# Reading the samples' states out four pairs of heads at a time instead of two

## The chip, the cores and the metric

The kernel runs on one core of a Trainium2 chip. The metric is the device time of one execution in microseconds (us): the median of the runs of a kernel on the chip. Times of single instructions come from one profiled execution.

## The reference, cut to what matters

The program is one step of a hybrid decoder layer, for a prompt of 1024 tokens and for 8 samples of 8 tokens each. It projects the normalised input, mixes one part over windows, passes the other through a state-space recurrence (SSD) with 32 heads in 4 groups, and joins both. The change concerns only the recurrence of the samples. For them a chunk is the 8 tokens of a sample, and the state that comes in is not zero:

```python
# per sample b, group g, head e (8 heads of a group share B and C); p: 64, n: 128
acs   = cumsum(dt * A)                                     # over the sample's 8 tokens
y     = einsum('bijge,bjgep->bigep', att, x)               # within the sample
y     = y + einsum('bign,bige,bgepn->bigep', C, exp(acs), h)     # read-out of the state h
last  = acs[:, -1]
w_in  = exp(last - acs) * dt
h     = h * exp(last) + einsum('bjgn,bjge,bjgep->bgepn', B, w_in, x)   # update of the state
```

The state h has 8 samples x 32 heads x 64 x 128 numbers (8.4 MB). Every state is read from memory once, read out with C, updated, and written back.

## The kernel before, in words

**The frame.** The weight products (gemms) are computed by a Strassen-like scheme. One `product` is twice 12 matmuls of 272 columns (L614) into a PSUM buffer `ps` or `mm`. The weights come in as tiles `rawA`, loaded on SP's queue; sums and differences of weight blocks are formed at L546, on DVE or on POOL (GpSimd); then each block is split into a high part `whi` (L165, ScalarE, that is ACT) and a low part `wlo` (L168, POOL), which go to the matmuls. Results are added up by DVE (L623), copied as `s` by ACT (L655), or passed through a sigmoid as `u` (L730) and stored as `gp` (L732).

**The samples' part** is the class `Samples`, one object for each of the 4 groups of 8 heads. A group's states come in 8 tiles `h`, j = 0 to 7: j divided by 4 says which four of the samples (the half), j modulo 4 which pair of heads. Each tile has 128 partitions (two heads x 64) and four blocks of 128 (four samples). For a tile there are these steps:

- `load_h0(j)`: load of the tile on SP's queue; there are four buffers.
- `turn(j)`: four transposes (L1309) into one PSUM buffer `ps` of four.
- `turned(j)`: ScalarE copies that to SBUF (L1314), into `hT` for an even j and `yt` for an odd one, one buffer each.
- `state(j)`: the read-out. For each of the four samples one matmul (L1323) takes the sample's C as weights (`cz`, 8 tokens padded to 32 columns) and the turned state, and writes 32 rows of the PSUM buffer `pc`. `pc` has one buffer, which takes the four pairs of a half side by side.
- `update(j)`: one matmul (L1332) of 96 rows and 512 columns gives what is added to the state, in a buffer `ps`; four DVE instructions (L1335) multiply the old state by its decay and add it, in place in `h`; the new state is stored from ACT's queue (L1337).

Once in a half, `out()` copies `pc` to SBUF (L1342, in the buffer `hT`), `end(hf)` turns it back and adds it to the result `t`, and `spread(hf)` and `split(hf)` (L1279 to L1293) prepare C, B and x for the four samples; the copy `cz` is among it (L1271). Once in a group, `decay()` masks the matrix `dec` on POOL (L1201, L1202) and takes eight exponentials of it on ScalarE (L1207), for which another function table is loaded than the one that the copies and the sigmoid use. `rows` (L1255 to L1257) and `within` give the part of the samples' own tokens.

**The order around it.** `all_samples()` is a generator that cuts these steps into 7 pieces for each group, with a `yield` between two. The pieces are put between the products of the last ten gemm units, at some pace (`samples_beside`, from L1658). PE (the matmul engine) and SP, whose queue does the loads, run in the order in which this is written; ACT, DVE and POOL run in an order that a scheduler makes when the program is built, from priorities and its own idea of when things are ready. The whole samples' part lies between about 600 and 800 us of the span. After it comes the recurrence of the prompt, and at the very end 16 loads on POOL's software queue that add the input to the result in memory (`plus_x`, L2048).

Of the kernel before, what the change touches and what calls it, by code (L numbers as in the profile page):

```python
# [20 lines left out]
P = 128  # L21
# [25 lines left out]
def tile_pool_ssd_step(  # L47
# [6 lines left out]
    nc = tc.nc  # L54
    uid = [0]

    def nm(s):
        uid[0] += 1
        return f"{s}_{uid[0]}"
# [177 lines left out]
    def x_copy(turned, eng):  # L237
        g3, k, px, c = turned
        o = BLK[g3][0]
        if eng is V:  # L240
            V.tensor_copy(tf[k][:, o:o + c], px[:, :c])
        else:
            act(tf[k][:, o:o + c], px[:, :c], AF.Copy)
# [981 lines left out]
    def spt(shape, tag, bufs, dt=F32):  # L1225
        return sp.tile(list(shape), dt, tag=tag, name=nm(tag), bufs=bufs)

    class Samples:
# [81 lines left out]
            self.pt[j] = pt  # L1310

        def turned(self, j):
            self.hts[j] = spt([P, 512], ("hT", "yt")[j % 2], 1)
            act(self.hts[j], self.pt.pop(j), AF.Copy)  # L1314

        def state(self, j):
# [40 lines left out]
    def all_samples():  # L1357
        gs_ = [Samples(g) for g in range(NG)]
        gs_[0].begin()
        gs_[0].decay()  # L1360
        for j in range(2):
            gs_[0].load_h0(j)
        yield
        gs_[0].rows()
        gs_[0].spread(0)
        yield
        gs_[0].split(0)
        yield
        for g, m in enumerate(gs_):
            n = gs_[g + 1] if g + 1 < NG else None  # L1370
            if g:
                gs_[g - 1].end(1)
            m.turn(0)
            m.turn(1)
            m.turned(0)
            m.turned(1)
            if g:
                m.split(0)
            m.within()
            m.load_h0(2)  # L1380
            m.load_h0(3)
            yield
            m.turn(2)
            m.turn(3)
            m.state(0)
            m.state(1)
            m.turned(2)
            m.turned(3)
            m.update(0)
            m.update(1)  # L1390
            m.load_h0(4)
            m.load_h0(5)
            yield
            m.state(2)
            m.state(3)
            m.out()
            m.update(2)
            m.update(3)
            m.spread(1)
            yield  # L1400
            m.end(0)
            m.turn(4)
            m.turn(5)
            m.turned(4)
            m.turned(5)
            m.split(1)
            m.load_h0(6)
            m.load_h0(7)
            if n:
                n.begin()  # L1410
            yield
            m.turn(6)
            m.turn(7)
            m.state(4)
            m.state(5)
            m.turned(6)
            m.turned(7)
            m.update(4)
            m.update(5)
            if n:  # L1420
                n.load_h0(0)
                n.load_h0(1)
                n.decay()
            yield
            if n:
                n.rows()
                n.spread(0)
            m.state(6)
            m.state(7)
            m.out()  # L1430
            m.update(6)
            m.update(7)
            yield
        gs_[-1].end(1)
        yield
# [220 lines left out]
    run_units(units, 1, lambda: next(pre, None))  # L1656
    banks_[0] = (PB, PA)
    side = all_samples()  # L1658
    due, made_ = [0.0], [0]
    FIRST = 14  # L1660
# [567 lines left out]
```

## Time and profile before

| | |
|---|---|
| runs of the kernel before | 1266.97, 1267.12, 1267.76 us; median 1267.12 |
| span of the profiled execution | 1265.2 us |
| its instructions | 26432 |
| busy: PE (matmul) | 1239.8 us, 98% |
| busy: PEld (weight load) | 1158.1 us, 92% |
| busy: DVE | 974.4 us, 77% |
| busy: ACT (ScalarE) | 682.6 us, 54% |
| busy: POOL (GpSimd) | 716.2 us, 57% |
| memory traffic | 171.26 MB read, 85.10 MB written, 203 GB/s over the span |

The span runs from the first to the last recorded instruction of the profiled execution. A run's time holds the launch too: the median of the runs is 1.9 us above the span. A line of the timeline gives the start in us from the span's start, the busy time in us, the engine, the source line, the operation with its output and inputs, its shape, and how many equal instructions in a row it stands for (x8); the busy time is that of the whole row. Square brackets at its end give an idle time ahead of it and the instruction that ended it. [...] A line of the waits gives who waited for what, the total idle time, the number of waits and the longest.

### The profile page before, as it was taken

The numbers are of one execution on the slowest core, as the hardware profiler recorded it, in microseconds if no ns is written. First come the engines' busy times: TensorE is split into PE (matmuls) and PEld (weight loads), VectorE is DVE, ScalarE is ACT, GpSimd is POOL, SyncE is SP. The second block draws the span as 40 slices with busy tenths as digits, with TensorE's granted clock in tenths as the row PEclk, the third lists the DMA queues.
The fourth block names the chain that finished last, engine by engine and source line by source line (L and its number), as shares of the span: only waits on it lengthen the run. The fifth ranks groups of instructions, "written<-read, shape, count | busy, mean of one in ns | idle before, by whom it ended". The sixth has DMA issues, their size and how long they took to land.

```text
span 1265.2 us, 26432 instructions
## 1 busy us (share of the span) xinstructions
PE 1239.8 (98%) x9679; PEld 1158.1 (92%) x9679; DVE 974.4 (77%) x1713; ACT 682.6 (54%) x1566; POOL 716.2 (57%) x607
## 2 busy tenths in 40 slices
PE   7999999999999999999999999999999999999997
PEld 6779999999999999999999989998888988999886
DVE  4686689986998598876676775488677988759986
ACT  4665347465556546455656554646676656401425
POOL 1006767886968777764444444354686877503662
PEclk9999999999999999999999999999999999999999
DMA  9836554564546545444666565998878887866884
GB/s 328 265 112 205 152 158 155 180 205 157 162 154 199 160 155 176 131 150 122 175 177 194 166 178 154 324 308 274 253 241 288 279 250 247 275 226 219 250 192 158
DMA packets 262499, 257.99 MB, mean 204 GB/s; under 512 B 29761, under 2 KB 200337, under 8 KB 262362
## 3 DMA queue, kind: packets, MB, share of 16 engines
q1 hardware_dynamic: 181632, 163.93, 42.7%
q10 hardware_dynamic: 78434, 88.18, 20.2%
q0 software_dynamic: 2304, 4.20, 1.8%
q8 instruction: 77, 1.26, 0.4%
q14 instruction: 52, 0.43, 0.1%
HBM read 171.26 MB, written 85.10 MB: 203 GB/s over the span
## 4 chain that ended last, share of the span: by engine, by line
PE 65%; DMA 2%; DVE 2%; ACT 1%; issue 1%; POOL 0%; SPq 0%; ACTq 0%; DVEq 0%
PE mm L358 17%; PE mm L614 14%; PE ps L614 14%; PE ps L1219 3%; PE pc L614 2%; PE pc L1541 2%; PE ps L1222 2%; PE ps L2023 2%; PE ps L2025 2%; PE ps L2024 2%; PE ps L1309 1%; PE ps L1516 1%; PE ps L1332 1%; PE pc L1323 1%; PE mm L2033 1%
## 5 line engine op out<-in xcount | busy, mean ns | idle before, releaser
L168 POOL TENSOR_TENSOR wlo<-rawA,whi 128x512 fp32r<-128x512 f32 x120 | 174.2, 1456 | 175.2 <-ACT whi L165 89.8
L168 POOL TENSOR_TENSOR wlo<-raw,whi 128x512 fp32r<-128x512 f32 x92 | 153.2, 1674 | 106.9 <-ACT whi L165 75.3
L358 PE MATMUL mm<-Y,whi 128*128 128x352 f32 (+1 forms) x960 | 196.2, 334 | 0.3 <-DVE Y L1579 0.3
L358 PEld LDWEIGHTS mm<-Y,whi 128*128 128x128 f32 x960 | 159.1, 188 | 6.6 <-issue 5.1
L1062 DVE SCALAR_TENSOR_TENSOR GA<-GA,cvT,GA 128x1112 f32<-128x1112 f32 x72 | 133.4, 1857 | 0.1
L614 PE MATMUL mm<-Y,whi 128*128 128x272 f32 x832 | 125.3, 292 | 1.5 <-DVE Y L484 1.1
L614 PE MATMUL ps<-Y,whi 128*128 128x272 f32 x832 | 122.4, 289 | 0.0
L165 ACT ACTIVATE whi<-rawA 128x512 fp32r<-128x512 f32 x125 | 78.1, 627 | 76.0 <-PE ps L614 42.1
L165 ACT ACTIVATE whi<-raw 128x512 fp32r<-128x512 f32 x96 | 59.4, 628 | 106.4 <-DVE raw L546 48.4
L614 PEld LDWEIGHTS mm<-Y,whi 128*128 128x128 f32 x832 | 112.1, 188 | 4.8 <-DVE Y L484 1.5
L614 PEld LDWEIGHTS ps<-Y,whi 128*128 128x128 f32 x832 | 110.9, 188 | 0.4
L1207 ACT ACTIVATE dec<-dec,acT 128x128 f32<-128x128 f32 (+1 forms) x288 | 86.9, 383 | 27.0 <-POOL dec L1198 26.4
L358 PE MATMUL mm<-Y,wlo 128*128 128x352 f32 (+1 forms) x480 | 98.7, 327 | 0.0
L358 PEld LDWEIGHTS mm<-Y,wlo 128*128 128x128 f32 x480 | 81.7, 188 | 0.0
L434 POOL TENSOR_TENSOR pw<-pw,ph 128x512 fp32r<-128x512 f32 x40 | 68.4, 1711 | 12.6 <-ACT ph L432 11.5
L614 PE MATMUL mm<-G,whi 128*128 128x272 f32 x496 | 73.4, 289 | 0.0
L614 PE MATMUL ps<-G,whi 128*128 128x272 f32 x496 | 72.6, 288 | 0.0
L614 PE MATMUL mm<-Y,wlo 128*128 128x272 f32 x416 | 69.3, 288 | 0.0
L614 PE MATMUL ps<-Y,wlo 128*128 128x272 f32 x416 | 69.2, 288 | 0.0
L614 PEld LDWEIGHTS mm<-G,whi 128*128 128x128 f32 x496 | 66.6, 189 | 0.7
L614 PEld LDWEIGHTS ps<-G,whi 128*128 128x128 f32 x496 | 66.3, 188 | 0.0
L1478 POOL TENSOR_TENSOR Y<-xb,Y 128x512 fp32r<-128x512 f32 x32 | 41.7, 1304 | 37.0 <-ACT Y L1476 37.0
(531 smaller groups left out, 3192.5 us busy)
## 6 DMA issues: line engine op xcount, KB each, us to landing
rawA<-in_w_in SPq DMA_DIRECT2D x62, 512.0 KB
dec<-acs_d SPq DMA_DIRECT2D x32, 512.0 KB
xbc<-GA ACTq DMA_DIRECT2D x24, 512.0 KB
Y<-wo SPq DMA_DIRECT2D x10, 1024.0 KB
pw<-in_w_ssm_out ACTq DMA_DIRECT2D x32, 256.0 KB
ws<-ph ACTq DMA_DIRECT2D x32, 256.0 KB
ws<-pw ACTq DMA_DIRECT2D x32, 256.0 KB
h<-in_state_ssm SPq DMA_DIRECT2D x32, 256.0 KB
```

The source lines that it names most:

```text
L165: ins = act(hi[:, :, :ncols], raw[:, :, :ncols], AF.Copy)
L168: (eng or nc.gpsimd).tensor_tensor(lo[:, :, :ncols], raw[:, :, :ncols], hi[:, :, :ncols].bitcast(F32), ALU.subtract)
L358: mm(ps[:, :n], w[k // 4][h][:, k % 4, :], r[k][:, o:o + n], start=(j == 0), stop=(j == len(terms) - 1))
L434: nc.gpsimd.tensor_tensor(raw.bitcast(F32R), raw, hi.bitcast(F32), ALU.subtract)
L614: mm(p, w[j // 8][:, k], A(k, s)[j // 4 == 1], start=(j == 0), stop=(j == 11))
L1062: V.scalar_tensor_tensor(d[:, :n], rp[:, k:k + n], cvT[:, 24 * k + mc:24 * k + mc + 1], d[:, :n], ALU.mult, ALU.add)
L1207: act(dec[:, h], dec[:, h], AF.Exp, bias=acT[:S, c, 8 * g + h:8 * g + h + 1], scale=-1.0)
L1219: mm(o[hh], xd[:S, 2 * q + hh, :], dec[:S, 2 * q + hh], start=True, stop=state is None)
L1222: mm(o[hh], state[:, h * 64:h * 64 + 64], cE[:, h], start=False, stop=True)
L1478: nc.gpsimd.tensor_tensor(yl[g][:, :, o:o + S], v, yhc.bitcast(F32), ALU.subtract)
L1541: mm(pu, bt, xw.rearrange("p h d -> p (h d)"), start=True, stop=True)
L2023: mm(ps, hi, y[:, k, c0:c0 + cw], start=(first and k == 0), stop=False)
```

## The change

There are four buffers of turned states instead of two: `turned(j)` takes `hT`, `yt`, `hU`, `hV` in turn. The read-out `state(j)` of the first two pairs of a half no longer stands between the transposes of the second two and their copies; it stands at the start of the next piece, together with that of the second two, so that 16 read-out matmuls follow one another. The two new buffers take 2 KB of each partition each; the scratch memory for transfers with software-made descriptors (those of POOL's software queue) goes from its 16384 bytes to 8192.

```diff
@@ turned(self, j)
-            self.hts[j] = spt([P, 512], ("hT", "yt")[j % 2], 1)
+            self.hts[j] = spt([P, 512], ("hT", "yt", "hU", "hV")[j % 4], 1)
             act(self.hts[j], self.pt.pop(j), AF.Copy)
@@ all_samples(), first half
             yield
             m.turn(2)
             m.turn(3)
-            m.state(0)
-            m.state(1)
             m.turned(2)
             m.turned(3)
             m.update(0)
...
             yield
-            m.state(2)
-            m.state(3)
+            for j in range(4):
+                m.state(j)
             m.out()
             m.update(2)
             m.update(3)
@@ all_samples(), second half
             yield
             m.turn(6)
             m.turn(7)
-            m.state(4)
-            m.state(5)
             m.turned(6)
             m.turned(7)
             m.update(4)
...
                 n.spread(0)
-            m.state(6)
-            m.state(7)
+            for j in range(4, 8):
+                m.state(j)
             m.out()
@@ kernel(**inputs)
-    nc = _bacc.Bacc("TRN2", target_bir_lowering=False, num_devices=1)
+    nc = _bacc.Bacc("TRN2", target_bir_lowering=False, num_devices=1, dynamic_dma_scratch_size=8192)
```

## The prediction

> **What bounds the kernel now.** I read the page first, then the busy time by stretch around the changed code, then who waited for whom on TensorE (PE) there, and last the timeline of single places.
>
> ```profile
> span 1265.2 us, 26432 instructions
> PE 1239.8 (98%) x9679; PEld 1158.1 (92%) x9679; DVE 974.4 (77%) x1713; ACT 682.6 (54%) x1566; POOL 716.2 (57%) x607
> 720.00:760.00 40.00, 38.27 (x352) 35.85 (x352) 29.59 (x70) 22.19 (x48) 18.21 (x15) 1.00 0.59 173
> PE ps L1332 <- ACT s L655: 2.0, 2, 1.7
> ```
>
> PE is busy for 98% of the span, so a microsecond of PE time is a microsecond of the end. The third row is one 40 us stretch of the part in which the samples' read-out runs (columns: length; PE, PEld, DVE, ACT, POOL busy; PE's granted clock): PE lacks 1.73 us there, and the fourth row, the waits of PE from 600 to 800 us, tells what for: PE waits in this whole part for one thing only, at L1332 (the update of the states) for ScalarE's copy `s` of L655, twice. So what counts is PE's own time, and these two places, which I call A (near 646 us, first group of heads) and C (near 735 us, third group). The three runs' median is 1267.12 us, 1.9 us over the span; I add my sum to the span and carry the 1.9 us along.
>
> **The change on PE.** There are 4 groups with two halves, so 8 places where the read-out of two pairs (L1323, 32 columns wide) disappears and 8 where it comes twice as long. A place of the first kind, PE's timeline at A, with the later one of the same half:
>
> ```profile
> 635.98 1.03 PE L1309 MATMUL ps<-ident,h 128*128 128x128 f32 x8
> 636.94 0.43 PE L1323 MATMUL pc<-hT,cz 128*32 128x128 f32 x8
> 637.18 0.40 PE L1323 MATMUL pc<-yt,cz 128*32 128x128 f32 x8
> 637.52 0.73 PE L1332 MATMUL ps<-dec 96*128 96x512 f32 x2
> 638.08 1.16 PE L614 MATMUL mm<-Y,whi 128*128 128x272 f32 x8
> ...
> 645.48 0.49 PE L1332 MATMUL ps<-dec 96*128 96x512 f32 x1
> 646.23 0.50 PE L1332 MATMUL ps<-dec 96*128 96x512 f32 x1 [0.25 <-ACT s L655]
> ```
>
> The eight transposes of L1309 start 0.108 us apart (1.03 less the 0.27 of one, by 7), the last at 636.74. From there to the next gemm matmul at 638.08 are 1.34 us. Without the read-out the update would follow the transposes at their pitch, about 0.11, and two matmuls of 512 columns stream at the gemm's rate: eight of 272 columns start (1.16 - 0.29) / 7 = 0.124 apart (0.29 is that of one), so 512 columns take 0.23, two 0.47. That is 0.57, and 0.77 us go. The difference holds two gaps at the change of array form, from 636.74 to 636.94 and from the last read-out, near 637.3, to 637.52. What comes back at the later place: sixteen narrow matmuls, which go four side by side; the first eight start 0.24 before the second eight (636.94 to 637.18), and at the transposes' pitch four more rounds take 4 x 0.108 = 0.43; bounds 0.43 and 0.48. Net 0.77 - 0.43 = 0.34 us gained in each half; 0.28 to 0.42 over the bounds, the upper one if a matmul follows a transpose at once. I take 0.34, by the pitches of the rows themselves.
>
> The freed 0.77 us only counts if the update isn't late for something else. Its second PSUM buffer was last read by ScalarE or VectorE after the gemm before it. The tightest of the eight places is the second group's first half:
>
> ```profile
> 658.82 0.43 DVE L623 TENSOR_TENSOR u<-u,ps 128x272 f32<-128x272 f32 x1
> 659.80 0.73 PE L1332 MATMUL ps<-dec 96*128 96x512 f32 x2
> ```
>
> The addition is over at 659.25. The second update matmul starts at 660.03 or later (the two take 0.73, one at most 0.50 by the rows above): 0.78 us of room, of which 0.77 are used up. If it doesn't fit, hundredths of a microsecond are lost. The buffers of the transposes are freed by ScalarE's two copies `turned`; these waited for the read-out (hT's and yt's old content) and now have buffers hU, hV of their own, so they come earlier.
>
> **The change on ScalarE.** PE and SP stand in the written order, ACT, DVE and POOL in the scheduler's. In the built program the new order on ACT differs at A and C in one thing that matters. Before: copies of the turned states, table load, seven exponentials `dec`, store of the updated state (`out<-h`), one exponential, second store. After: copies, **first store**, table load, eight exponentials, second store, and then as before the halving `whi`, the second table load, `u` twice, `s` of `mm`, `whi`, `s` of `ps`. The store is issued from ACT's queue and waits there for DVE's update L1335; behind it now stand the table load and all exponentials, and at the end the copy `s` that PE waits for. In the second group both stores stand ahead of the table load already, and PE doesn't wait there, where no copy `s` holds its buffer. ACT and DVE at A before:
>
> ```profile
> 638.59 1.28 ACT L1207 ACT_TABLE_LOAD   x1
> 639.88 0.35 ACT L1207 ACTIVATE dec<-dec,acT 64x64 f32<-64x64 f32 x1
> 639.99 0.40 ACTq L1337 DMA_DIRECT2D out<-h  x1
> ...
> 641.02 0.40 ACTq L1337 DMA_DIRECT2D out<-h  x1
> ...
> 641.82 0.62 ACT L165 ACTIVATE whi<-rawA 128x512 fp32r<-128x512 f32 x1
> 642.45 1.28 ACT L730 ACT_TABLE_LOAD   x1
> 643.75 0.75 ACT L730 ACTIVATE u<-u 128x272 f32<-128x272 f32 x2
> 644.52 0.34 ACTq L732 DMA_DIRECT2D gp<-u  x1
> 644.97 0.40 ACT L655 ACTIVATE s<-mm 128x272 f32<-128x272 f32 x1 [0.48 <-PE ps L1257]
> 645.26 0.62 ACT L165 ACTIVATE whi<-rawA 128x512 fp32r<-128x512 f32 x1
> 645.78 0.39 ACT L655 ACTIVATE s<-ps 128x272 f32<-128x272 f32 x1
> 636.53 2.39 DVE L546 TENSOR_TENSOR rawA<-rawA,rawA 128x512 f32<-128x512 f32 x1
> 638.85 2.14 DVE L1335 SCALAR_TENSOR_TENSOR h<-h,E,ps 128x128 f32<-128x128 f32 x8
> ```
>
> The store is issued at 639.99, when the first four of the eight L1335 are done, and its issue takes 0.40: the table load starts near 640.46 instead of 638.59. From there: load 1.28, eight exponentials 1.94 (639.88 to 641.82), `whi` 0.63 to the load, load 1.30, `u` twice 0.75 to 646.37. The store of `u` now stands behind `s` of `mm`, not ahead of it, so only `whi` waits for its issue: it starts 0.45 after `u` as `s` did (644.50 to 644.97), then 0.52 to `s` of `ps` and 0.39 for it. Sum 7.3 us: `s` ends at 647.76, and PE goes on 0.06 later (before: 645.78 + 0.39 to 646.23), at 647.8. That is **1.6 us later than now**, whatever PE saved on its way there. The DVE chain isn't moved: L1335 already waits for the addition L546, not for PE. At C:
>
> ```profile
> 729.36 0.40 ACTq L1337 DMA_DIRECT2D out<-h  x1
> 729.80 0.35 ACT L1207 ACTIVATE dec<-dec,acT 64x64 f32<-64x64 f32 x1 [0.53 <-DVE h L1335]
> 734.88 0.39 ACT L655 ACTIVATE s<-ps 128x272 f32<-128x272 f32 x1
> 721.65 0.86 DVE L546 TENSOR_TENSOR raw<-raw,rawA 128x512 f32<-128x512 f32 x1
> 724.14 4.15 DVE L546 TENSOR_TENSOR rawA<-rawA,rawA 128x512 f32<-128x512 f32 x1
> 728.21 2.14 DVE L1335 SCALAR_TENSOR_TENSOR h<-h,E,ps 128x128 f32<-128x128 f32 x8
> 733.09 0.49 PE L1332 MATMUL ps<-dec 96*128 96x512 f32 x1
> 735.32 0.50 PE L1332 MATMUL ps<-dec 96*128 96x512 f32 x1 [1.73 <-ACT s L655]
> 724.16 1.27 POOL L168 TENSOR_TENSOR wlo<-raw,whi 128x512 fp32r<-128x512 f32 x1
> 725.39 1.10 POOL L1202 TENSOR_SCALAR_AFFINE_SELECT dec<-dec 64x512 f32<-64x512 f32 x1
> 726.46 1.28 POOL L168 TENSOR_TENSOR wlo<-raw,whi 128x512 fp32r<-128x512 f32 x1
> 727.71 1.74 POOL L546 TENSOR_TENSOR raw<-raw,rawA 128x512 f32<-128x512 f32 x1
> ```
>
> One exponential already waits for the store here (the 0.53). The store at 729.36 puts the table load at 729.82, 7.3 us later `s` ends at 737.12, PE goes on at 737.2 instead of 735.32: **1.9 us later**.
>
> **The sum.** Six halves gain 0.34 each, -2.0 us; A +1.6, C +1.9: +1.5 us. 1265.2 + 1.5 + 1.9 = **1268.6 us**. The six other halves' savings pass on in full, as PE waits for nothing else there. The terms' bounds (0.28 to 0.42 for a half, 0.2 for each stall) give this case 1267.8 to 1269.3. Costed at nothing: the second store at A, which leaves near 642.05 instead of 641.02, behind the eighth exponential; SP's next load into that buffer waits for its landing, but PE needs it only after another product of 24 matmuls, and those are late by the same stall. The delayed `whi` of A and C feed products that come two and more later. On DVE the copy `cz` now stands ahead of L1335 at these places, behind the stall; only stores wait for that.
>
> The 8 KB scratch serves POOL's own transfers, the 16 adding loads `plus_x` at the very end (packets, MB, share of 16 engines):
>
> ```profile
> q0 software_dynamic: 2304, 4.20, 1.8%
> ```
>
> No row shows a wait for its space; if half of it were too little, transfers issued in a burst would wait for earlier ones to land. I take nothing.
>
> **Rivals.** (1) *The additions L546 come out short, and it gets faster.* The addition takes 0.86 us when left alone (721.65), 2.39 at A and 4.15 at C, where it starts as POOL begins an operation and ends only in POOL's fourth. If both were at 0.86, L1335 would start 1.5 us sooner at A and 3.3 sooner at C, and the chain behind it: A +0.1, C -1.4, in sum -3.3 and 1263.8 us. Against it: DVE and POOL keep their order up to there, and what starts them moves with PE alike.
>
> (1b) *The addition waits for one POOL operation only.*
>
> ```profile
> 635.96 1.27 POOL L168 TENSOR_TENSOR wlo<-raw,whi 128x512 fp32r<-128x512 f32 x1
> ```
>
> With the operation that runs when it comes (over at 637.23 at A, 725.43 at C) and its own 0.86 it would end at 638.09 and 726.29, 0.8 and 2.0 us sooner than in these rows: A +0.8, C -0.1, in sum -1.3 and 1265.8 us. Only the 4.15 at C, which outlasts three operations, speaks against it. [...]
>
> (2) *Slower: the addition at A takes as long as at C.* Then L1335 and the store come 1.76 us later there, and A costs 3.4 instead of 1.6: 1270.4 us. It decides from about 3.4 us of that addition on.
>
> (3) *Slower: PE cools down.* At C PE would stand idle from about 733.2 to 737.2, 4.0 us; now it is 1.73, with a clock of 1.00 in the stretch around it. If PE ran at half its rate for as long as the pause was, 2.0 us were lost: 1270.6 us. It decides from a length of pause between 1.73 and 4.0 us. [...]
>
> (4) *The scratch is too small.* POOL's loads at the end come late; slower by a few us.
>
> (5) *ACT isn't held by the store's wait*: eight halves gain 0.34, A and C stay as they are: 8 x 0.34 is -2.7, 1264.4 us, and less if ACT comes sooner too. The 0.53 us row at C speaks against it.
>
> **How the numbers follow.** 0.2% (2.5 us) is about what a measurement of this kernel can tell from no change: 1264.6 to 1269.7 counts as the same. Forecast 0.42, rival 1b and other mixed outcomes 0.10: same 0.52. Rival 2 0.15, rival 3 0.13, rival 4 0.03: slower 0.31. Rival 1 0.11, rival 5 0.06: faster 0.17. The range reaches from rival 1's 1263.8 less 0.4 for its terms' bounds to rival 3's 1270.6 with 0.4 more: 1263.4 to 1271.0. Left out are both slow rivals at once, the scratch, and the lower end of rivals 1 and 5.
>
> **What would show it.** L1332 straight behind L1309 without gap, about 0.57 us to the next gemm matmul; L1323 in sixteen-fold groups; PE's waits at L1332 for `s` growing from 2.0 us to some 5.5, two times; on ACT at A and C the first `out<-h` ahead of the table load, with about 2 us idle before it. It is wrong if PE doesn't wait longer at L1332, if the addition L546 before A or C has another length, or if a new place shows up where PE waits.

## The result: slower

The changed kernel took 1276.05 us (median of 7 runs, 1271.33 to 1280.62), the kernel before beside it 1267.76 us (7 runs, 1262.66 to 1271.42): a ratio of 1.0065, 95% interval 1.004 to 1.009. Run again later beside the experiments it took 1276.37 us against 1270.98, a ratio of 1.0031 (1.0004 to 1.0058). Both intervals lie above 1; forecast were 1268.6 us and 1271.0 at most. The runs of one kernel lie up to 15 us apart, and the long ones have the lower mean clock of PE (0.990 in the changed kernel's run of 1280.62 us, 0.998 in that of 1271.33); in the profiles the granted clock falls from 1.00 to 0.50 for 3.4 us at a time or 6.8 (ahead of the last 20 us of the span), at other places in each execution: near 56, 736, 821 and 1128 us in the changed kernel's first, near 365, 651 and 744 us in its second. The mean clock over the changed kernel's 19 runs is 0.9938, over 103 runs of before 0.9959; at 1270 us the difference is worth 2.7 us (an estimate: it counts half clock in idle time too).

The profiled execution of the changed kernel: the page's first lines, and PE's waits from 600 to 850 us (total, times, longest).

```profile
span 1273.7 us, 26430 instructions
PE 1244.5 (98%) x9679; PEld 1165.4 (91%) x9679; DVE 974.9 (77%) x1713; ACT 682.3 (54%) x1566; POOL 716.7 (56%) x607
PE ps L1332 <- ACT s L655: 5.6, 2, 4.7
PE mm L358 <- DVE R L1728: 2.4, 1, 2.4
```

The span grew by 8.5 us, PE's busy time by 4.7. The waits for `s` grew from 2.0 to 5.6 us (foretold were "some 5.5"), and a wait that was not foretold stands beside them: 2.4 us for `R`, behind the samples' part.

PE's timeline at A after the change:

```profile
636.82 1.03 PE L1309 MATMUL ps<-ident,h 128*128 128x128 f32 x8
637.61 0.70 PE L1332 MATMUL ps<-dec 96*128 96x512 f32 x2
638.15 1.16 PE L614 MATMUL mm<-Y,whi 128*128 128x272 f32 x8
...
644.96 0.43 PE L1323 MATMUL pc<-hT,cz 128*32 128x128 f32 x8
645.21 0.40 PE L1323 MATMUL pc<-yt,cz 128*32 128x128 f32 x8
645.42 0.40 PE L1323 MATMUL pc<-hU,cz 128*32 128x128 f32 x8
645.64 0.40 PE L1323 MATMUL pc<-hV,cz 128*32 128x128 f32 x8
645.97 0.51 PE L1332 MATMUL ps<-dec 96*128 96x512 f32 x1
647.36 0.50 PE L1332 MATMUL ps<-dec 96*128 96x512 f32 x1 [0.88 <-ACT s L655]
```

The update follows the transposes without the two gaps: from the last transpose (636.82 + 7 x 0.108 = 637.58) to the next gemm matmul it is 0.57 us, as costed. The four groups of eight read-outs start 0.21 to 0.25 apart. So PE's own work did what was expected. The second update then waits for `s`.

What happened at C: ScalarE, DVE, POOL and PE there after the change, and in the last line the POOL instruction before it. ACTq is the issue of a transfer by ScalarE; its row can overlap the engine's other rows (in the prediction's rows at A, an issue from 639.99 to 640.39 us beside an exponential from 639.88 to 640.23).

```profile
730.38 0.40 ACTq L1337 DMA_DIRECT2D out<-h  x1
730.86 1.28 ACT L1207 ACT_TABLE_LOAD   x1 [5.02 <-DVE h L1335]
732.41 1.76 ACT L1207 ACTIVATE dec<-dec,acT 64x64 f32<-64x64 f32 x7
737.71 0.38 ACT L655 ACTIVATE s<-ps 128x272 f32<-128x272 f32 x1
724.36 4.95 DVE L546 TENSOR_TENSOR rawA<-rawA,rawA 128x512 f32<-128x512 f32 x1
729.24 2.14 DVE L1335 SCALAR_TENSOR_TENSOR h<-h,E,ps 128x128 f32<-128x128 f32 x8
724.10 1.09 POOL L1201 TENSOR_SCALAR_AFFINE_SELECT dec<-dec 64x512 f32<-64x512 f32 x1 [1.91 <-DMA dec<-acs_d]
728.73 1.74 POOL L546 TENSOR_TENSOR raw<-raw,rawA 128x512 f32<-128x512 f32 x1
738.14 0.79 PE L1332 MATMUL ps<-dec 96*128 96x512 f32 x1 [4.68 <-ACT s L655]
738.74 2.02 PE L614 MATMUL mm<-Y,whi 128*128 128x272 f32 x8
723.09 1.10 POOL L1201 TENSOR_SCALAR_AFFINE_SELECT dec<-dec 64x512 f32<-64x512 f32 x1 [1.12 <-DMA dec<-acs_d]
```

ScalarE stands idle for 5.02 us ahead of the table load, because the store ahead of it waits for L1335, which stands on DVE behind an addition of 4.95 us that began 0.26 us after POOL's first of five operations and ended in the fifth. In the kernel before it began 1.05 us after that first operation and took 4.15. In both the addition ends 5.2 us after POOL's first operation began (at 728.29 and 729.31), and that operation comes 1.01 us later now, because its load of `dec` lands later. From the table load to the end of `s` it is 7.23 us (7.3 were forecast), and PE goes on 0.05 us later. And behind the wait eight gemm matmuls take 2.02 us instead of 1.16. The busy time by stretch shows why (columns: length; PE, PEld, DVE, ACT, POOL; the granted clock is the last but two):

```profile
734.00:738.00 4.00, 0.00 (x0) 0.00 (x0) 2.80 (x7) 3.83 (x9) 1.38 (x2) 0.73 0.61 179
738.00:742.00 4.00, 3.86 (x16) 3.76 (x17) 1.37 (x5) 0.58 (x2) 1.16 (x1) 0.50 0.69 162
742.00:746.00 4.00, 4.00 (x44) 3.82 (x43) 2.19 (x5) 1.23 (x2) 1.28 (x1) 0.91 0.70 205
```

PE did nothing for 4.7 us, from 733.46 on. The 0.73 of the first row puts the fall of the clock near 735.8, 2.4 us into the wait; PE then ran at half clock until 742.7. The third place, the first chunk of the prompt's recurrence; DVE and PE after, and the same DVE instruction before in the last line:

```profile
820.24 0.69 DVE L1525 TENSOR_TENSOR xw<-ps,wdT 128x512 f32<-128x512 f32 x1 [4.88 <-DMA gs<-u]
820.84 1.41 DVE L1728 TENSOR_TENSOR R<-mm,R 128x384 f32<-128x384 f32 x3
821.45 1.65 PE L358 MATMUL mm<-Y,whi 128*128 128x384 f32 x4 [2.36 <-DVE R L1728]
811.05 0.68 DVE L1529 TENSOR_TENSOR xw<-ps,wdT 128x512 f32<-128x512 f32 x1
```

The write of `xw` waits 4.88 us for the store of the gemms' last result `u`, which has nothing to do with it. The reason given is that the tile now lies where `u` lay; no trace shows an address, but the experiments below tie the wait to the size of the scratch. Behind it stand three results `R` that PE's buffers wait for.

Where the 8.5 us of this pair of traces are, from the starts of the same gemm matmul in both:

| | us |
|---|---|
| up to 616 us (a stretch of half clock at 56 to 60, and 0.5 at the start; nothing that the change touches) | +1.1 |
| eight short read-outs gone, 0.72 to 0.78 each | -6.0 |
| eight read-outs longer, 0.44 each | +3.5 |
| longer wait at A (0.88 for 0.25) | +0.6 |
| longer wait at C (4.68 for 1.73) | +3.0 |
| half clock behind C | +2.0 |
| wait for `R` | +2.4 |
| half clock behind it | +1.6 |
| from there to the end (a wait of before at 1065 gone, half clock at 1128) | +0.3 |

### The profile page after: what moved, and what is told of

Its sections match the earlier page's. It is cut to its first block, busy times and chain, and to the rows that moved or that the text cites. A ratio compares the mean times of both kernels' runs of the same rounds, so it can differ in the third digit from the quotient of the medians.

```text
span 1273.7 us, 26430 instructions
## 1 busy us (share of the span) xinstructions
PE 1244.5 (98%) x9679; PEld 1165.4 (91%) x9679; DVE 974.9 (77%) x1713; ACT 682.3 (54%) x1566; POOL 716.7 (56%) x607
## 4 chain that ended last, share of the span: by engine, by line
PE 63%; DMA 3%; DVE 2%; issue 1%; ACT 1%; POOL 1%; SPq 0%; ACTq 0%; POOLq 0%; DVEq 0%
PE mm L358 17%; PE mm L614 14%; PE ps L614 13%; PE ps L1219 2%; PE pc L614 2%; PE pc L1537 2%; PE ps L1222 2%; PE ps L2019 2%; PE ps L2021 2%; PE ps L2020 2%; PE ps L1309 1%; DMA xb<-xbc 1%; PE ps L1512 1%; PE ps L1332 1%; DMA R<-in_w_o 1%
```

## The experiments

All twelve were timed in five rounds beside the kernel before on the same chip (its medians there: 1271.02, 1270.98 and 1270.30 us). Ratios are to it, with their 95% intervals; a ratio is estimated from all runs and is not the quotient of the two medians (1276.37 to 1270.98 above gives 1.0042 beside the ratio of 1.0031), so what is said "by the medians" is rough. Six of the profiles with the regrouped read-out show a further wait of PE, 0.7 us near 700 us for VectorE's `tn`, which the changed kernel's first profile does not have.

**Scratch alone** (on the kernel before):

```diff
-    nc = _bacc.Bacc("TRN2", target_bir_lowering=False, num_devices=1)
+    nc = _bacc.Bacc("TRN2", target_bir_lowering=False, num_devices=1, dynamic_dma_scratch_size=8192)
```

> The kernel before with only the scratch of 8192 bytes, nothing else changed. My theory: a smaller scratch moves all the tiles that are placed behind it, and the first tile xw of the prompt's recurrence then comes to lie where the last results u2 and u3 of the gemms wait to be stored; so DVE's first write of xw waits for two stores, and PE behind it. I expect one new wait of PE of about 2.4 us for R (near 815 us), 2.4 to 4 us more than before in all (1270 to 1272 us against 1267.8), and PE's waits for s as before, 2.0 us. Rival (the scratch costs nothing, all of the loss comes from the samples' part): within 0.5 us of before, no such wait. Second rival (the scratch is too small for POOL's loads): a loss behind 1250 us.

1272.44 us, 1.0017 (0.9994 to 1.004). DVE and PE's wait in its profile:

```profile
818.63 0.69 DVE L1529 TENSOR_TENSOR xw<-ps,wdT 128x512 f32<-128x512 f32 x1 [3.99 <-DMA gs<-u]
PE mm L358 <- DVE R L1732: 1.5, 1, 1.5
```

The same wait of `xw` on the store of `u`, with no read-out and no buffer changed: it comes from the scratch's size alone. PE loses 1.5 us by it here, less than the 2.4 expected. Behind 1250 us nothing is lost: from PE's last matmul to the end it is 7.6 us, as before. The total of 1.4 us by the medians is below the 2.4 to 4 expected, and its interval holds zero; shown is the wait, not its share in the time.

**Scratch of 12288 in the changed kernel** (`8192` to `12288`).

> The changed kernel with a scratch of 12288 bytes instead of 8192, which is what two more buffers of 2 KB leave. The first xw then waits for another, earlier store (s). My theory: that store has landed or nearly, so the wait of 2.4 us at R goes; 2.4 to 4 us less than the changed kernel, 1272 to 1273.6 us, and the waits for s stay at 5 to 6 us. Rival (placement is not the cause): 1276 us as changed.

1274.35 us, 1.0041 (1.0018 to 1.0064).

```profile
817.42 0.68 DVE L1525 TENSOR_TENSOR xw<-ps,wdT 128x512 f32<-128x512 f32 x1
PE ps L1332 <- ACT s L655: 6.5, 2, 4.4
```

`xw` runs without a wait, no PE wait for `R` is left, and the kernel is still slower, so placement is not the only cause. How much it costs isn't shown: by the medians 3.3 us above before are left here (expected were 1272 to 1273.6 us), but the ratio is no lower than the 1.0031 of the changed kernel's second measurement.

**Exponentials ahead of the stores**, in the changed kernel (the lines that matter; `last` is handed through `exps`, `decay` and `update`):

```diff
-            m.update(4)
-            m.update(5)
+            last = n.decay() if n else None       # returns the eighth exponential
+            m.update(4, last)                     # issues its store behind `last`
+            m.update(5, last)
             if n:
                 n.load_h0(0)
                 n.load_h0(1)
-                n.decay()
```

> The changed kernel (scratch 8192) with both stores of tiles 4 and 5 issued only after the eighth exponential of the next group, so that ScalarE doesn't stand with table load and exponentials behind the first store. My theory: the wait for s at A goes (0.9 to 0), the one at C goes from 4.7 to about 2.7, because the second store still waits for L1335 there, and PE keeps its full clock at C; the wait for R stays. 5 us less than the changed kernel, about 1271 us. Rival (the long addition L546 sets the end of s, not the order on ScalarE): A and C stay within 0.5 us, 1276 us.

1271.19 us, 0.9995 (0.9974 to 1.0015); the line numbers here are up to three higher.

```profile
PE ps L1333 <- ACT s L655: 1.8, 1, 1.8
725.17 4.22 DVE L546 TENSOR_TENSOR rawA<-rawA,rawA 128x512 f32<-128x512 f32 x1
```

A is gone and C down to 1.8 us (2.7 were expected), although the addition L546 still took 4.22 us: the rival falls. By the medians five microseconds come back from the order of two stores on ScalarE, though the interval overlaps the 1.0004 to 1.0058 of the changed kernel's second measurement. The wait for `R` was 1.3 us. PE's clock fell behind C all the same in this profile (0.50 from 737 to 739 us), against the expectation.

**Both at once.**

> Both at once: scratch of 12288 bytes, and the stores of tiles 4 and 5 behind the eighth exponential. My theory: what is left is the gain of the longer read-out, 8 x 0.34 = 2.7 us, less 1 us more of waiting at C, so about 1266 us against 1267.8 before. Rival (the regrouped read-out itself costs something that I haven't seen): above before, 1269 us or more.

1269.67 us, 0.999 (0.9971 to 1.001). PE waits 0.9 us for `s`. By the medians 1.35 us are gained where 1.8 were expected, not to be told from nothing. In its profile the addition at C was short:

```profile
722.68 0.68 DVE L546 TENSOR_TENSOR rawA<-rawA,rawA 128x512 f32<-128x512 f32 x1
723.06 1.27 POOL L1201 TENSOR_SCALAR_AFFINE_SELECT dec<-dec 64x512 f32<-64x512 f32 x1 [2.54 <-DMA dec<-acs_d]
```

POOL's chain starts when the load of `dec` lands. Here it landed 0.38 us after the addition had begun; in the changed kernel's first profile 0.26 us before it, and the addition took 4.95.

**The changed kernel again.**

> The changed kernel once more, beside the same runs of the kernel before as the three others. By the four runs so far (scratch alone +1.4 us, scratch of 12288 with the new order on ScalarE +3.3) it should be 4.7 us above before, a ratio of 1.0037; if the two causes strengthen each other, up to 8 us (1.0065). PE's waits for s of 5.5 to 6.5 us and one for R of 1.5 to 2.4.

1276.37 us, 1.0031 (1.0004 to 1.0058): +5.4 us by the medians. Its waits for `s` are longer than in the first profile, because the addition at A took 2.40 us and not 1.14; the wait at A was 2.13, and PE ran at half clock behind it (0.50 from 652 to 655 us):

```profile
PE ps L1332 <- ACT s L655: 6.8, 2, 4.6
639.30 2.40 DVE L546 TENSOR_TENSOR rawA<-rawA,rawA 128x512 f32<-128x512 f32 x1
650.54 0.50 PE L1332 MATMUL ps<-dec 96*128 96x512 f32 x1 [2.13 <-ACT s L655]
648.00:652.00 4.00, 1.87 (x11) 1.51 (x12) 2.38 (x11) 2.83 (x7) 1.73 (x2) 0.98 0.66 203
652.00:656.00 4.00, 4.00 (x23) 4.00 (x23) 0.96 (x3) 0.63 (x1) 0.28 (x1) 0.60 0.82 202
```

**Work for PE during the wait at C** (the read-out of the same half five times more; the lines that matter):

```diff
-            for j in range(4, 8):
-                m.state(j)
+            for again in range(6 if g == 2 else 1):
+                for j in range(4, 8):
+                    m.state(j, again)
```

> The changed kernel with the read-out of the third group's second half done six times instead of once, into the same place with the same result, so that PE works during about 4.4 us of its wait at C instead of standing idle; the wait of the second update for s stays where it is. Theory (the idle time of 4.7 us at C lets PE's clock fall to half for some us behind it): no low clock between 733 and 745 us in the profile, the gemm matmuls behind C at 0.12 us each, and 1.5 to 2 us less than the changed kernel. Rival (the low clock comes whatever PE does there): the same time as the changed kernel, or up to 0.5 us more.

1274.94 us, 1.0028 (1.0006 to 1.0051).

```profile
744.10 0.50 PE L1332 MATMUL ps<-dec 96*128 96x512 f32 x1 [0.39 <-ACT s L655]
744.44 1.16 PE L614 MATMUL mm<-Y,whi 128*128 128x272 f32 x8
744.00:748.00 4.00, 3.90 (x31) 3.86 (x32) 2.63 (x10) 1.17 (x3) 1.22 (x2) 1.00 0.60 155
```

The update comes at the same point of the chain, and behind it the clock is 1.00 and the gemm at full pace (1.16 us for eight matmuls; 2.02 in the changed kernel's two profiles): with 0.39 us of idle PE at C instead of 4.68 and 4.64 the clock did not fall there. The 1.4 us that the median lies below the run above are near the expected 1.5 to 2, but the intervals overlap.

**Exponentials earlier**, scratch 12288: `n.begin()` at the end of the third piece instead of the fourth, and `n.decay()` at the end of the fourth instead of the fifth. In the program that is one piece earlier for each (the expectation below says two); in the profile the exponentials ahead of A run at 619.9 us instead of 641.4.

```diff
             m.spread(1)
+            if n:
+                n.begin()
             yield
...
             if n:
-                n.begin()
+                n.decay()
             yield
...
                 n.load_h0(1)
-                n.decay()
             yield
```

> Scratch of 12288 bytes, and the next group's dec is loaded and exponentiated two pieces earlier (begin at the end of the third piece, decay at the end of the fourth), so that the table load and the eight exponentials stand ahead of PE's waits A and C. My theory (the order on ScalarE at A and C sets the end of s): PE waits there for nothing, not even the 2.0 us of before; 2.7 + 2.0 us less than before, a ratio of 0.9965. Rival (DVE's and POOL's exclusion at C sets it): 1 us or more of waiting for s stays. Second rival: the exponentials now hold another copy that PE waits for, and the gain is lost at a new place.

1265.23 us, 0.9954 (0.9934 to 0.9975). PE's waits from 600 to 850 us, all of them:

```profile
PE mm L358 <- DVE Y L1576: 0.3, 1, 0.3
```

It waits for `s` nowhere. With POOL's masks gone from there the addition at C took 1.10 us. The gain is larger than the 0.9965 expected, which lies in the interval.

**Stores of tiles 4 and 5 from SP's queue**, scratch 12288:

```diff
-            store_(new_ssm_s[0, 4 * hf:4 * hf + 4, ...
+            (load if j in (4, 5) else store_)(new_ssm_s[0, 4 * hf:4 * hf + 4, ...
```

> Scratch of 12288 bytes, and tiles 4 and 5 are stored from SP's queue instead of ScalarE's, so that ScalarE waits for no update L1335 ahead of the exponentials. My theory: waits for s at A none, at C under 0.5 us; 2.7 + 1.5 us less than before, a ratio of 0.997. Rival (the stores hold SP's queue, and the loads behind them come late): a new wait for rawA or for h, and no gain.

1265.14 us, 0.9949 (0.993 to 0.9969).

```profile
724.67 3.90 DVE L546 TENSOR_TENSOR rawA<-rawA,rawA 128x512 f32<-128x512 f32 x1
726.17 1.28 ACT L1207 ACT_TABLE_LOAD   x1
733.02 0.38 ACT L655 ACTIVATE s<-ps 128x272 f32<-128x272 f32 x1
733.27 0.73 PE L1332 MATMUL ps<-dec 96*128 96x512 f32 x2
```

The addition is long as ever (3.90), but ScalarE no longer waits for what comes of it, `s` ends 0.13 us after PE's first update starts, and both updates run without a pause. At A the addition took 4.03 us, and PE waits for no `s` there either. The gain is larger than the 0.997 expected, which lies just outside the interval. Of the rival's waits for `rawA` or `h` there is none.

**The order alone**, in the kernel before: `n.decay(first)`, whose exponentials are issued behind the first store of tile 4 (the lines that matter).

```diff
-            m.update(4)
+            first = m.update(4)                   # returns its store
...
-                n.decay()
+                n.decay(first)                    # exponentials behind it
```

> The kernel before, with two buffers, the old read-out and the old scratch; only the eight exponentials at the end of each group are issued behind the first store of tile 4, which gives ScalarE the order of the changed kernel at A and C. My theory (this order is the main part of the loss): PE's waits for s grow from 2.0 us to 5.5 to 6.5, PE's clock falls behind C in the profile, 3.5 to 5.5 us more than before, a ratio of 1.003 to 1.0045. Rival (the order costs only where the read-outs are regrouped too): within 1 us of before.

1275.53 us, 1.0038 (1.0023 to 1.0053).

```profile
644.16 1.28 ACT L1207 ACT_TABLE_LOAD   x1 [3.46 <-DVE h L1336]
PE ps L1333 <- ACT s L655: 6.6, 2, 3.3
```

(Line numbers are one higher here.) Without any other part of the change, its order on ScalarE costs 5.2 us by the medians, within what was expected, and its interval lies clear of 1. PE's clock fell to 0.50 with both waits of 3.3 us (from 651 to 657 us and from 747 to 749). The addition at A took 3.95 us here.

**The stores on SP's queue, in the kernel before.**

> The kernel before, only that tiles 4 and 5 are stored from SP's queue. It tells apart what of the 5.8 us that this gained in the regrouped kernel belongs to the regrouped read-out. My theory: here the waits for s of 2.0 us go, and 2 to 2.5 us with them, a ratio of 0.998; the rest, about 3 us, is the read-out's. Rival (the store's queue brings nearly all of it, the read-out nothing): a ratio of 0.995 to 0.996.

1268.30 us, 0.9985 (0.9968 to 1.0003); waits for `s` 0.7 us, where none was expected. So of the 5.8 us that the same edit is below before in the regrouped kernel, 2.0 are the queue's and 3.8 the read-out's, by the medians (the two were timed on different chips); the traces' own sum for the read-out is 6.0 - 3.5 = 2.5. The rival's ratio of 0.995 to 0.996 lies outside the interval.

**Both remedies.**

> The changed kernel with a scratch of 12288 bytes, exponentials two pieces earlier, and tiles 4 and 5 stored from SP's queue. By my theory PE has no wait left at A and C in either of the two, so both together are worth no more than one: a ratio of 0.9945 to 0.9955. Rival (the stores still hold ScalarE somewhere): 1 us less than that.

1264.33 us, 0.9957 (0.9942 to 0.9973): no more than one of them. PE waits for `s` in none of the three profiles.

**All stores on SP's queue.**

> The changed kernel with a scratch of 12288 bytes, and all eight tiles of a group stored from SP's queue, so that ScalarE waits for no update of a state anywhere. PE waits for nothing of these stores with tiles 4 and 5 alone on SP, so I expect the same time as with these two, a ratio of 0.995; rival (SP's queue becomes the bound: its loads wait behind the stores): a new wait for rawA or h and 1 us or more back.

1267.30 us, 0.997 (0.9955 to 0.9985), by the median 2 us behind tiles 4 and 5 alone. In its profile PE waits again a little at L1332 and for a load of `h`:

```profile
PE ps L1332 <- ACT s L655: 0.6, 1, 0.6
PE ps L1309 <- DMA h<-in_state_ssm: 0.3, 1, 0.3
```

The intervals overlap, so the rival is not shown. This program's ScalarE waits for no store of a state, and it gains no more than the one with two stores moved. Three of these versions (1264.3 to 1265.2 us) beat both the kernel before and the changed one.

## Why the prediction was wrong

- **Right: PE's own work.** 0.77 us gone and 0.43 added in each half were forecast; 0.72 to 0.78 and 0.44 are in the traces, -2.5 us net for -2.7. The read-out four pairs at a time is a gain, in the traces and, by the medians, with the stores on SP's queue (3.8 us).
- **Right: ScalarE's order as a cost, and the largest.** With the half clock behind C it makes 5.6 of the 8.5 us. Its chain of 7.3 us was 7.23, and the order alone, put into the kernel before, makes 1.0038. Rival (5), that ScalarE isn't held by the store, falls: it stood idle for 5.02 us ahead of the table load. Rival (4) did not occur either: from PE's last matmul to the end it is 7.65 us before and after.
- **Size of A and C.** The prediction's own times give waits of 2.2 us at A (645.64 to 647.8) and 4.0 at C, 6.2 in all; its "some 5.5" leaves out that PE comes 0.34 us sooner to each. At A 0.88 and in the second execution 2.13 were found, as the addition L546 took 1.14 and 2.40 us. That the first profile's 5.6 us lie near 5.5 is luck: A came out shorter and C longer. At C it was 4.68 and 4.64, with the addition at 4.95 and 4.92. The sentence that "the DVE chain isn't moved" failed there, as POOL's operations had moved by 1.01 us. At C the addition took 0.68, 2.71, 3.90, 4.22, 4.66, 4.92, 4.95 and 5.06 us in the eight profiles with the new read-out and POOL's masks at their old place, and 3.92 to 4.19 in the four with the old one. Taking the length over from the kernel before was a guess.
- **What the addition hung on.** POOL sets its end: of 14 additions at A and C that began 0.15 to 1.31 us after POOL's first mask operation (L1201), 13 ended 5.20 to 5.23 us after that operation began. The nine at A that began 1.4 to 1.8 us after it ended 2.9 to 4.1 us after it, and the one that began ahead of it took 0.68 us. So it matters when the load of `dec` lands, with which POOL's operations start. Rival (1), short at both places, didn't occur in the changed kernel, nor did rival (2). What rival (1b) says of one operation did, at A in the first profile:
```profile
636.69 1.27 POOL L168 TENSOR_TENSOR wlo<-raw,whi 128x512 fp32r<-128x512 f32 x1
637.38 1.14 DVE L546 TENSOR_TENSOR rawA<-rawA,rawA 128x512 f32<-128x512 f32 x1
637.92 1.55 POOL L1202 TENSOR_SCALAR_AFFINE_SELECT dec<-dec 64x512 f32<-64x512 f32 x1
```

  DVE's addition ended 0.56 us after the POOL operation that ran when it began (637.96 to 638.52), and POOL's next took 1.55 us instead of the 1.09 at C. At C it outlasted four operations of POOL's and ended at 729.31, in the fifth.
- **The first step that failed: the half clock behind C stood in rival (3), with a chance of 0.13, and was put at nothing in the sum.** It is a consequence of the forecast: the forecast's 4.0 us of idle PE at C had to carry a price for the clock. Worked out for the rival were 2.0 us; measured were 2.0. Filling the wait with work took the fall away (a clock of 1.00 behind C, 0.39 us of waiting). That the price agrees is luck: it was to be half the length of the pause, which was the author's assumption, but the stretches of half clock lasted 3.4 us or twice that, and not as the pause is long (6.8 at C in the first profile, 2.3 of it within the wait, but 3.4 in the second behind nearly the same wait; 3.4 also behind the wait of 2.36 for `R`, and behind A in the second profile, where 0.98 and 0.60 over 4 us each, above, make 0.2 + 3.2).
- **The second step that failed: "I take nothing" for the scratch.** The prediction looked at whose transfers use it, not at what moves when it shrinks. In all five profiles with 8192 bytes the first `xw` waits for the store of `u`, for 2.3 to 4.9 us; PE then waits 2.4 and 2.0 us for `R` in the changed kernel's two profiles, 1.3 and 0.3 in two of its variants and 1.5 in the kernel before with the scratch alone. With 12288 bytes `xw` waits at most 0.8 us, for another store (`s`), and PE for no `R`. That the tile lies where `u` lay is a reading of the built program, with which this agrees. In the first profile a half clock behind the wait for `R` cost 1.6 us more.
- **The range** ended at 1271.0. Two slow rivals at once and the scratch were left out of it; the longer C, the clock and the placement came together in one kernel. Of the 7.0 us between the forecast's +1.5 and this pair's +8.5, the wait for `R` with the half clock behind it makes 4.0, the half clock behind C 2.0, the longer C 0.7, the time up to 616 us 1.1, the shorter A -1.3; 0.5 is left for the rest.

What is not settled is how the 8.3 and 5.4 us divide among the causes: only the order on ScalarE stands clear of zero by itself. Nor is it settled why the addition ended behind one of POOL's operations at one place and behind four at another.

## What to carry to other kernels

A regrouping that saves work on the engine that bounds the kernel also moves the other engines' instructions: read the new order of each of them, and look for an instruction that waits (here a store on ScalarE's queue) and now stands ahead of a chain that the bounding engine waits for. Where an edit frees or takes memory, list which transfer each first write behind it now waits for. And if a forecast for a kernel like this one says that PE stands idle for 2 us or more, the price of a slower clock belongs in the forecast itself: here, between 600 and 850 us, the clock fell to 0.50 with 9 of the 10 waits of 2.0 us or more.

## What the runs showed of the hardware

In the changed kernel's first profile PE's clock fell to half 2.4 us into the wait of 4.68 at C (1.00 up to 735.5 us, 0.86 from there to 736, 0.50 after it). At the three places between 600 and 850 us, over all profiles: behind waits of 3.3 us or more the clock fell in 5 cases of 5, behind 2.0 to 2.4 us in 4 of 5, behind 1.3 to 1.8 in 1 of 5, behind shorter ones never. Outside that part it is less clear: near 363 us it fell behind the waits of 2.2 us in three profiles (the changed kernel's second, that with work for PE at C, that with all stores on SP's queue), between 1059 and 1073 us behind one of 3.1 but neither of two of 2.4 and 2.6, and near 56 us, where PE has short pauses of 1.3 us at most, in 6 of 13 profiles (that of the scratch alone not counted). It also fell with no wait at all, in the changed kernel behind 18 matmuls of one column:

```profile
1125.85 2.05 PE L1889 MATMUL ps<-ones,sq_acc 128*128 128x1 f32 x18
1128.00:1132.00 4.00, 4.00 (x15) 4.00 (x16) 1.49 (x7) 0.35 (x2) 0.00 (x0) 0.57 1.05 402
```

The same matmuls were followed by a clock of 1.00 in the kernel before and in the changed kernel's second profile; over all 14 profiles the clock fell behind them in 5. As two executions of one program differ in this, something that the program doesn't set takes part; what it is, no run here shows. A stretch of 3.4 us at half clock costs 1.7 us when PE has work all through it (an estimate, half of its length; behind the wait for `R` 1.6 were measured), so a wait of 2 us that is followed by one costs nearly twice its own length.
